# Hybrid encoder trunk, one core: a token-major projection behind every convolution projection

## The chip, the core and the metric

The kernel runs on one core of one Trainium2 chip, in one launch. The metric is the device time of one execution in microseconds, as the median of the runs; less is better. Work is spread over TensorE (PE in the profile, its weight loads PEld), VectorE (DVE), ScalarE (ACT), GpSimd (POOL) and the queue of SyncE (SP), which only issues DMAs here.

## What is computed

Two layers (DEPTH 2) over 256 tokens of width 1024. Each layer normalises its input, projects it with one wide matrix, runs two token mixers on pieces of the projection, and joins them:

```python
for l in range(DEPTH):
    h = rmsnorm(x, norm_w[l])
    proj = h @ w_in[l]
    (q_a, k_a, v_a, ab_a, z_a, q_b, k_b, v_b, z_b,
     gate_a, gate_b) = jnp.split(proj, SPLIT_IDX, axis=-1)
    y_a = gated_delta_branch(q_a, k_a, v_a, ab_a, z_a, conv_w[l], a_log[l], dt_bias[l], gdn_norm_w[l])
    lambda_init = 0.8 - 0.6 * math.exp(-0.3 * l)
    y_b = diff_attention_branch(q_b, k_b, v_b, z_b, cos, sin, diff_lambda[l], diff_subln_w[l], lambda_init)
    merged = (jax.nn.sigmoid(gate_a) * (y_a @ w_pa[l])
              + jax.nn.sigmoid(gate_b) * (y_b @ w_pb[l]))
    x = x + merged @ w_out[l]
return rmsnorm(x, final_norm_w)
```

The first branch (a) sends q, k and v through a convolution of 5 taps along the tokens and a SiLU, and runs a gated delta rule in both directions. In chunked form that rule needs, for every head and chunk, the inverse of a unit triangular matrix:

```python
L = jnp.where(strict, jnp.einsum('bhncd,bhnmd->bhncm', kb, k) * decay, 0.0)
T = lax.linalg.triangular_solve(eye + L, jnp.broadcast_to(eye, L.shape),
                                left_side=True, lower=True, unit_diagonal=True)
```

The second branch (b) rotates part of q and k (rotary positions), takes the difference of two softmax attentions per head, and multiplies by v.

## The kernel before, in words

**Projections.** All of them use the normalised input held transposed in `hT` as a high and a low float32r part, and weights that are split on the chip: per tile of 256 rows by 512 columns, SP issues a load of 512 KB into `raw`, ACT casts it to `hi` (L223), and DVE forms the rest `lo` (L225). `raw` has three buffers, `hi` and `lo` two each, so a weight tile can be made only two tiles ahead of PE. Three products (hi by hi, hi by lo, lo by hi) make one result. There are two forms. `proj_fm` (L279, feature-major, called by `conv`) has the weights stationary: 96 matmuls of 128x256 (L289, L291, L293) into the tiles `pf_k`, `pf_q` or `pf_v`, for 512 channels. `proj_tm` (L230, token-major) has the tokens stationary: 48 matmuls of 128x512 (L237 to L239) into tiles named `pp_...`, for 512 columns.

**After a convolution projection** DVE has much to do: for each of four blocks of 128 channels ACT scales the middle tap (L508), DVE adds the four other taps straight out of PSUM (L512, four instructions, tiles `cvk`, `cvq`, `cvv`), ACT takes a tanh (L516, `thk`, `thv`), DVE forms the SiLU (L521), and PE turns the result token-major (L529, `ctk`, `ctq`, `ctv`). A PSUM bank is given back only when the taps of both its blocks are added. **After a token-major projection** there is less: v's half (`vb_part`) is two copies on ACT (L343, out of `pp_vb`); q and k of branch b (`qk_part`, arguments: 0 for q or 1 for k, and the half of the heads) are a copy on ACT (L439, `stg`), four small rotations on DVE (L444 to L447) and transposes (L450, `qkt`), twice.

**PSUM.** The accumulators of projections and the attention scores share four banks (tag `p`, `banks2`); each projection and each head takes two.

**The chain of the triangular inverse.** With k's norms known, `log_decays` and `decays` make the decays; `weigh_k` forms A out of them and of k's products (L596, L620); `turn_blocks` sends A's diagonal blocks through DRAM; after q's second half `take_blocks` (L649) turns one copy of them on DVE, and `substitute` runs 31 dependent steps of two DVE instructions each (L655, L656, tiles `fstmp` and `X`). `spread_blocks` then copies the result on DVE (L659, `lt`), GpSimd writes it to DRAM (L663) and reads it back into the places that PE needs (L685 tile `T`, L689 tile `U_`), and `merges` builds the full inverse from the 32x32 blocks on PE (L703 `y64p`, L715 `zt`, L720 `z`, then L737 and L745), for two groups of four heads. `chunks` uses it.

**Heads of branch b.** `head(h)` makes scores on PE (L816, tiles `sc`, two banks, one for each of the two softmaxes), maxima on DVE (L823, `mx`), exponentials on ACT (L825, `es`), their difference on DVE (L828 to L833), transposes (L836, `at`) and the product with v (L842, `av`). Between them stand the projections `z_part` (tiles `pp_zb` and `pp_za`), whose result DVE takes through L304; then come the gates `pp_gb`, `pp_ga` and the products `pp_pb`, `pp_pa`.

**What sets the order.** The body of a layer is a list of calls written by hand (L859 to L900). A scheduler then orders the instructions of each engine when the program is built, by the order of the calls and by modelled times, so that pieces of later calls come ahead where it finds room; it also picks the banks and buffers. On the chip every engine's list runs in that fixed order. The first token-major half of v stands ahead of the list (`proj_by_tile`, L357).

Of the kernel before, what the change touches and what calls it, by code (L numbers as in the profile page):

```python
# [50 lines left out]
def hybrid_encoder(  # L51
# [178 lines left out]
    def proj_tm(act, w, c0, n, evac, nm, places=(None,) * 4):  # L230

        accs = banks2(f"pp_{nm}")
        for kt, hi, lo in weights(w, c0, n, nm, places):
            for m in range(NM):
                ts_ = slice(m * P, (m + 1) * P)
                o = accs[m][:, :n]
                T.matmul(o, act[kt // 4][:, 0, kt % 4, ts_], hi, start=kt == 0, stop=False)  # L237
                T.matmul(o, act[kt // 4][:, 0, kt % 4, ts_], lo, start=False, stop=False)  # L238
                mark["proj"] = T.matmul(o, act[kt // 4][:, 1, kt % 4, ts_], hi, start=False,  # L239
                                        stop=kt == KT - 1).ins  # L240
        for m in range(NM):
            evac(m, accs[m][:, :n])
# [91 lines left out]
    for l in range(DEPTH):  # L334
# [6 lines left out]
        def evac_v(i):  # L341
            def evac(m, ps):
                S.copy(vb[i][:, m, :], ps)  # L343
            return evac
# [111 lines left out]
        def vb_part(i):  # L456
            proj_tm(hT, wl, C_VB + 512 * i, 512, evac_v(i), f"vb{l}{i}")
# [164 lines left out]
        def weigh_q(g, c):  # L622
            bv = B[:, c, 4 * g : 4 * g + 4]
            V.tensor_tensor(bv, gram("kq", g, c, 1).unsqueeze(2).to_broadcast([P, 4, 2, P]), bv, ALU.mult)
# [21 lines left out]
        def take_blocks():  # L646

            with tc.issue_after(mark["conv"]):
                V.tensor_copy(la[64:P], lt[64:P].rearrange("p j i -> p i j"))  # L649
# [207 lines left out]


        conv("k", C_KA, 0, 0)  # L859
        conv("k", C_KA, 0, 1)  # L860
        vb_part(1)
        log_decays()
        conv("q", C_QA, 1, 0)
        qk_part(0, 0)
        decays(0, 0)
        weigh_k(0, 0)
        decays(0, 1)
# [7 lines left out]
        weigh_q(0, 1)  # L875
        conv("q", C_QA, 1, 1)
        take_blocks()
        qk_part(0, 1)
        weigh_q(1, 0)
        weigh_q(1, 1)  # L880
        substitute(0, 31)
        spread_blocks()
        conv("v", C_VA, None, 0)
        qk_part(1, 0)
        conv("v", C_VA, None, 1)
        qk_part(1, 1)
        head(0)
        z_part(zb, C_ZB, "zb", 0)
        head(1)
# [143 lines left out]
```

## Time and profile before

| quantity | value |
|---|---|
| median of 3 runs | 797.72 us (795.93 to 799.87) |
| span of the profiled execution | 798.2 us |
| what lies around it | the span is 0.5 us above the median of the runs |
| instructions | 13819 |
| moved by DMA | 126.92 MB |
| first layer's convolution stage, k's first group to the first head | about 28 to 177 us |
| second layer's | about 422 to 570 us |

Times within the trace are counted from the start of the span. A busy share is an average over stages; an engine's idle time is put down, in the view of waits, to what released it. An instruction's duration includes its latency: matmuls that follow each other overlap, and DVE's instructions begin some 0.08 us before the one ahead of them is shown to end.

### The profile page before, as it was taken

The numbers are of one execution on the slowest core, as the hardware profiler recorded it, in microseconds if no ns is written. First come the engines' busy times: TensorE is split into PE (matmuls) and PEld (weight loads), VectorE is DVE, ScalarE is ACT, GpSimd is POOL, SyncE is SP. The second block draws the span as 40 slices with busy tenths as digits, with TensorE's granted clock in tenths as the row PEclk, the third lists the DMA queues.
The fourth block names the chain that finished last, engine by engine and source line by source line (L and its number), as shares of the span: only waits on it lengthen the run. The fifth ranks groups of instructions, "written<-read, shape, count | busy, mean of one in ns | idle before, by whom it ended". The sixth has DMA issues, their size and how long they took to land.

```text
span 798.2 us, 13819 instructions
## 1 busy us (share of the span) xinstructions
PE 766.4 (96%) x5224; PEld 654.0 (82%) x5224; DVE 559.3 (70%) x1054; ACT 478.5 (60%) x1043; POOL 109.5 (14%) x149
## 2 busy tenths in 40 slices
PE   8989999999998999999989899999999999999996
PEld 4989889887876888878769798799778789887875
DVE  5487878999972653476655977889999436546564
ACT  5458776556775745654534786765667586446443
POOL 6000471100050100100010014501001401001000
PEclk9999999999998999999999999999999999999999
DMA  7455756554484544355754566566455734344551
GB/s 205 152 167 158 224 158 200 172 161 130 133 212 87 158 139 126 107 171 184 234 156 135 153 179 222 159 173 181 134 159 150 194 109 158 115 128 125 188 190 74
DMA packets 65842, 126.92 MB, mean 159 GB/s; under 512 B 7391, under 2 KB 7727, under 8 KB 65776
## 3 DMA queue, kind: packets, MB, share of 16 engines
q1 hardware_dynamic: 61198, 114.69, 47.4%
q0 software_dynamic: 4576, 11.35, 5.9%
q8 instruction: 41, 0.67, 0.4%
q14 instruction: 25, 0.20, 0.1%
q10 hardware_dynamic: 2, 0.00, 0.0%
HBM read 121.27 MB, written 4.75 MB: 158 GB/s over the span
## 4 chain that ended last, share of the span: by engine, by line
PE 66%; DVE 13%; DMA 9%; ACT 6%; issue 3%; POOL 3%; SPq 0%; POOLq 0%; ACTq 0%; DVEq 0%
PE pp_vb L274 3%; PE pp_qk L238 2%; PE pp_qk L239 2%; PE pp_qk L237 2%; DMA U__96<-udr 2%; PE pf_v L289 2%; PE pp_gb L237 2%; PE pf_v L293 2%; PE pf_v L291 2%; PE pp_gb L238 2%; PE pp_gb L239 2%; PE pp_pb L238 2%; PE pp_pb L237 2%; PE pp_pb L239 2%; PE pf_k L293 2%
## 5 line engine op out<-in xcount | busy, mean ns | idle before, releaser
L238 PE MATMUL pp_qk<-lo_qk,hT 128*128 128x512 f32 x128 | 51.3, 401 | 1.0 <-DVE lo_qk L225 1.0
L239 PE MATMUL pp_qk<-hi_qk,hT 128*128 128x512 f32 x128 | 50.1, 391 | 0.0
L237 PE MATMUL pp_qk<-hi_qk,hT 128*128 128x512 f32 x128 | 46.1, 398 | 1.1 <-ACT hi_qk L223 1.1
L225 DVE TENSOR_TENSOR lo_qk<-raw_qk,hi_qk 128x1024 fp32r<-128x1024 f32 x32 | 40.2, 1256 | 9.0 <-ACT hi_qk L223 8.7
L223 ACT CAST hi_qk<-raw_qk 128x1024 fp32r<-128x1024 f32 x32 | 33.5, 1046 | 20.0 <-PE pp_qk L239 10.8
L225 DVE TENSOR_TENSOR lo_pb<-raw_pb,hi_pb 128x1024 fp32r<-128x1024 f32 x16 | 19.6, 1224 | 33.6 <-ACT hi_pb L223 33.6
L289 PE MATMUL pf_q<-hT,hi_q 128*128 128x256 f32 x128 | 36.3, 288 | 1.3 <-ACT hi_q L223 1.2
L225 DVE TENSOR_TENSOR lo_gb<-raw_gb,hi_gb 128x1024 fp32r<-128x1024 f32 x16 | 19.6, 1223 | 25.2 <-ACT hi_gb L223 25.2
L289 PE MATMUL pf_v<-hT,hi_v 128*128 128x256 f32 x128 | 36.5, 288 | 0.0
L291 PE MATMUL pf_v<-hT,hi_v 128*128 128x256 f32 x128 | 36.2, 285 | 0.0
L825 ACT ACTIVATE es<-sc,mx 128x256 f32<-128x256 f32 x64 | 29.9, 475 | 10.4 <-DVE mx L823 10.3
L291 PE MATMUL pf_q<-hT,hi_q 128*128 128x256 f32 x128 | 35.8, 284 | 0.0
L289 PE MATMUL pf_k<-hT,hi_k 128*128 128x256 f32 x128 | 35.6, 283 | 0.0
L291 PE MATMUL pf_k<-hT,hi_k 128*128 128x256 f32 x128 | 35.6, 283 | 0.0
L293 PE MATMUL pf_q<-hT,lo_q 128*128 128x256 f32 x128 | 35.2, 290 | 0.1
L293 PE MATMUL pf_v<-hT,lo_v 128*128 128x256 f32 x128 | 34.6, 285 | 0.0
L293 PE MATMUL pf_k<-hT,lo_k 128*128 128x256 f32 x128 | 34.3, 286 | 0.0
L225 DVE TENSOR_TENSOR lo_pa<-raw_pa,hi_pa 128x1024 fp32r<-128x1024 f32 x16 | 19.6, 1224 | 17.9 <-ACT hi_pa L223 17.9
L225 DVE TENSOR_TENSOR lo_k<-raw_k,hi_k 128x1024 fp32r<-128x1024 f32 x16 | 19.6, 1222 | 17.6 <-ACT hi_k L223 17.6
L512 DVE SCALAR_TENSOR_TENSOR cvk<-pf_k,cw,cvk 128x254 f32<-128x254 f32 (+1 forms) x64 | 29.2, 478 | 2.0 <-ACT cvk L508 1.2
L223 ACT CAST hi_pa<-raw_pa 128x1024 fp32r<-128x1024 f32 x16 | 16.9, 1055 | 22.4 <-PE pp_pa L239 18.9
L223 ACT CAST hi_pb<-raw_pb 128x1024 fp32r<-128x1024 f32 x16 | 16.8, 1050 | 22.4 <-PE pp_pb L239 17.9
(367 smaller groups left out, 2550.6 us busy)
## 6 DMA issues: line engine op xcount, KB each, us to landing
raw_qk<-in_w_in_dram SPq DMA_DIRECT2D x32, 512.0 KB, 3.7
raw_vb<-in_w_in_dram SPq DMA_DIRECT2D x16, 512.0 KB, 4.1
raw_k<-in_w_in_dram SPq DMA_DIRECT2D x16, 512.0 KB, 3.8
raw_q<-in_w_in_dram SPq DMA_DIRECT2D x16, 512.0 KB, 3.7
raw_v<-in_w_in_dram SPq DMA_DIRECT2D x16, 512.0 KB, 4.0
raw_zb<-in_w_in_dram SPq DMA_DIRECT2D x16, 512.0 KB, 3.6
raw_za<-in_w_in_dram SPq DMA_DIRECT2D x16, 512.0 KB, 3.9
raw_gb<-in_w_in_dram SPq DMA_DIRECT2D x16, 512.0 KB, 4.4
```

What stands on the lines that cost most here:

```text
L223: S.copy(hi[:, :, :n], raw[:, :, :n])
L225: V.tensor_tensor(lo[:, :, :n], raw[:, :, :n], hi[:, :, :n].bitcast(F32), ALU.subtract)
L237: T.matmul(o, act[kt // 4][:, 0, kt % 4, ts_], hi, start=kt == 0, stop=False)
L238: T.matmul(o, act[kt // 4][:, 0, kt % 4, ts_], lo, start=False, stop=False)
L239: mark["proj"] = T.matmul(o, act[kt // 4][:, 1, kt % 4, ts_], hi, start=False, stop=kt == KT - 1).ins
L274: mark["proj"] = T.matmul(o, a_, w_, start=kt == 0 and a_ is ah and w_ is hi, stop=kt == KT - 1 and a_ is al).ins
L289: T.matmul(o, hi[:, cs], act[kt // 4][:, 0, kt % 4, :], start=first, stop=False, skip_group_check=True)
L291: T.matmul(o, hi[:, cs], act[kt // 4][:, 1, kt % 4, :], start=False, stop=False, skip_group_check=True)
L293: T.matmul(o, lo[:, cs], act[kt // 4][:, 0, kt % 4, :], start=False, stop=done, skip_group_check=True)
L512: V.scalar_tensor_tensor(ca[:, o0:o1], acc[:, b, o0 + sft : o1 + sft], cw[:, j, cb : cb + 1], ca[:, o0:o1], ALU.mult, ALU.add)
L825: S.activation(es[:, n, qt, :], spv[:, qt, :], AF.Exp, bias=mx[:, n, qt : qt + 1], accum_out=s_all[:, h, n, qt : qt + 1])
```

## The change

It moves four calls in the hand-written list, in both layers, and adds or removes no operation. v's second half goes from behind k's second group to between k's two groups. The rotated halves of q and k each go one place ahead: the first to behind k's second group, the others to between and behind q's and v's groups. Behind v's second group no token-major projection is left, and the first attention head follows it.

```diff
         conv("k", C_KA, 0, 0)
+        vb_part(1)
         conv("k", C_KA, 0, 1)
-        vb_part(1)
+        qk_part(0, 0)
         log_decays()
         conv("q", C_QA, 1, 0)
-        qk_part(0, 0)
+        qk_part(0, 1)
         decays(0, 0)
...
         conv("q", C_QA, 1, 1)
         take_blocks()
-        qk_part(0, 1)
+        qk_part(1, 0)
         weigh_q(1, 0)
         weigh_q(1, 1)
         substitute(0, 31)
         spread_blocks()
         conv("v", C_VA, None, 0)
-        qk_part(1, 0)
+        qk_part(1, 1)
         conv("v", C_VA, None, 1)
-        qk_part(1, 1)
         head(0)
```

The scheduler makes of it the following, in three places of the first layer; the second layer is alike. In names, `vb` is branch b's v, `k` is branch a's k, and numbers tell one buffer from another.

DVE, while the first group of k is taken out of PSUM (blocks `cvk_513` and `cvk_522` are its last two; `cvk_663` belongs to k's second group), before:

```order
L225 TENSOR_TENSOR lo_vb_740<-raw_vb_741,hi_vb_739 128x1024
L521 SCALAR_TENSOR_TENSOR kq_336<-thk_519,cvk_513 128x2x128
L512 SCALAR_TENSOR_TENSOR cvk_522<-pf_k_364,cw_274,cvk_522 128x254
L512 SCALAR_TENSOR_TENSOR cvk_522<-pf_k_364,cw_274,cvk_522 128x255
L512 SCALAR_TENSOR_TENSOR cvk_663<-pf_k_541,cw_274,cvk_663 128x254
L512 SCALAR_TENSOR_TENSOR cvk_522<-pf_k_364,cw_274,cvk_522 128x255
L512 SCALAR_TENSOR_TENSOR cvk_663<-pf_k_541,cw_274,cvk_663 128x255
```

And after (`lo_k_680` and `lo_k_710` are weights of k's second group, whose taps now come later):

```order
L225 TENSOR_TENSOR lo_k_650<-raw_k_651,hi_k_649 128x1024
L521 SCALAR_TENSOR_TENSOR kq_336<-thk_519,cvk_513 128x2x128
L512 SCALAR_TENSOR_TENSOR cvk_522<-pf_k_364,cw_274,cvk_522 128x254
L512 SCALAR_TENSOR_TENSOR cvk_522<-pf_k_364,cw_274,cvk_522 128x255
L225 TENSOR_TENSOR lo_k_680<-raw_k_681,hi_k_679 128x1024
L512 SCALAR_TENSOR_TENSOR cvk_522<-pf_k_364,cw_274,cvk_522 128x255
L512 SCALAR_TENSOR_TENSOR cvk_522<-pf_k_364,cw_274,cvk_522 128x254
L225 TENSOR_TENSOR lo_k_710<-raw_k_711,hi_k_709 128x1024
```

The taps of two groups no longer stand among each other; weights stand between them.

PE, where the last projection of the convolution stage ends and the first head and `z_part` begin, before (`sc_2116` holds the scores whose bank the second half of `pp_zb`'s accumulators takes over; the first takes a bank that `pp_qk` left):

```order
L238 MATMUL pp_qk_2014<-lo_qk_2070,hT_1_113 128x512
L239 MATMUL pp_qk_2014<-hi_qk_2069,hT_1_113 128x512
L816 MATMUL sc_2116<-qkT_0_298 128x256
L816 MATMUL sc_2115<-qkT_0_298 128x256
L816 MATMUL sc_2116<-qkT_0_298 128x256
L816 MATMUL sc_2115<-qkT_0_298 128x256
L237 MATMUL pp_zb_2147<-hi_zb_2149,hT_0_112 128x512
```

And after (one score stands further ahead, inside v's second group):

```order
L291 MATMUL pf_v_1944<-hT_1_113,hi_v_2035 128x256
L293 MATMUL pf_v_1944<-hT_1_113,lo_v_2036 128x256
L816 MATMUL sc_2115<-qkT_0_298 128x256
L816 MATMUL sc_2116<-qkT_0_298 128x256
L816 MATMUL sc_2115<-qkT_0_298 128x256
L529 MATMUL ctv_1837<-ident,thv_1834 128x128 x2
L237 MATMUL pp_zb_2147<-hi_zb_2149,hT_0_112 128x512
```

The head now follows v's second group, and both accumulators of `pp_zb` lie in banks that the head's scores hold; the built program puts `sc_2116` and `pp_zb_2147` into one bank.

PE, where the merges begin, before (`2501` and `2571` belong to the first group of heads, `2536` to the second):

```order
L703 MATMUL y64p_2536<-T_2490,A_346 32x32 x32
L715 MATMUL zt_2571<-U__96,y_2502 32x32 x2
L842 MATMUL av_2819<-vb_1_140,aT_2811 128x128 x4
L239 MATMUL pp_za_3016<-hi_za_3071,hT_1_113 128x512
L836 MATMUL at_3110<-ident,es_3093 128x128 x4
L715 MATMUL zt_2571<-U__96,y_2502 32x32 x30
L720 MATMUL z_2572<-y_2502,U__96 32x32 x16
L816 MATMUL sc_3130<-qkT_1_299 128x256
```

And after:

```order
L842 MATMUL av_2819<-vb_1_140,aT_2811 128x128
L238 MATMUL pp_za_3016<-lo_za_3072,hT_1_113 128x512
L239 MATMUL pp_za_3016<-hi_za_3071,hT_1_113 128x512
L836 MATMUL at_3110<-ident,es_3093 128x128 x4
L816 MATMUL sc_3130<-qkT_1_299 128x256
L816 MATMUL sc_3129<-qkT_1_299 128x256
L703 MATMUL y64p_2536<-T_2490,A_346 32x32 x32
L715 MATMUL zt_2571<-U__96,y_2502 32x32 x2
L842 MATMUL av_3119<-vb_1_140,aT_3111 128x128 x4
L720 MATMUL z_2572<-y_2502,U__96 32x32 x16
L237 MATMUL pp_gb_3218<-hi_gb_3220,hT_0_112 128x512
```

The product `av_2819`, the last of `pp_za`, the transposes `at_3110` and the last head's four scores (the piece leaves out their second pair) now stand ahead of the first `zt`, and 24 matmuls of `pp_gb` behind it.

## The prediction

> **What bounds the kernel now.** I read the page first, then PE's waits, then the stages by windows, then the places where PE waits, by the timeline. The page:
>
> ```profile
> span 798.2 us, 13819 instructions
> PE 766.4 (96%) x5224; PEld 654.0 (82%) x5224; DVE 559.3 (70%) x1054; ACT 478.5 (60%) x1043; POOL 109.5 (14%) x149
> PE 66%; DVE 13%; DMA 9%; ACT 6%; issue 3%; POOL 3%; SPq 0%; POOLq 0%; ACTq 0%; DVEq 0%
> raw_qk<-in_w_in_dram SPq DMA_DIRECT2D x32, 512.0 KB, 3.7
> ```
>
> PE is busy for 96% and the chain runs through it for 66%. The change leaves PE's work as it is, so it can only win or lose idle time and clock. Weights land in 3.7 us, and no wait below is on one: the four loads of a moved projection move with it in SP's queue and cost nothing. Where PE waits, over both layers:
>
> ```profile
> PE zt L715 <- DMA U__96<-udr: 3.3, 2, 1.9
> PE pp_vb L237 <- DVE cvk L512: 3.1, 2, 1.5
> PE y64p L703 <- DMA T<-udr: 2.8, 2, 2.5
> PE pp_vb L238 <- DVE lo_vb L225: 0.9, 2, 0.5
> PE pp_zb L237 <- ACT es L825: 0.9, 2, 0.5
> ```
>
> Two of the rows belong to v's second half behind both of k's groups: it wants the bank of k's first group, whose taps DVE has not yet read. The `zt` and `y64p` rows belong to the merges, which wait for the DMAs behind the substitution. Stages of 12 us (columns: time, busy PE, PEld, DVE, ACT, POOL, granted clock, DMA share, GB/s):
>
> ```profile
> 52.00:64.00 12.00, 9.85 (x47) 7.43 (x47) 10.84 (x22) 9.37 (x28) 0.00 (x0) 1.00 0.37 104
> 64.00:76.00 12.00, 12.00 (x90) 11.41 (x89) 9.06 (x15) 8.38 (x19) 0.00 (x0) 1.00 0.66 203
> 184.00:196.00 12.00, 12.00 (x63) 9.37 (x62) 11.48 (x21) 8.38 (x20) 0.00 (x0) 1.00 0.49 139
> ```
>
> The reader is to see two kinds of stage. At 52 to 64 PE loses 2.15 us. At 184 to 196, under the heads, PE loses nothing, but DVE is full, because the substitution fills it. DVE decides there when the copy `lt` comes, and with it T and U.
>
> **The change, part by part.**
>
> *1. v's half between k's groups.* Under each token-major projection DVE has room for the taps of the group ahead, and its bank has been free for a whole projection. Both `pp_vb` rows should go: 4.0 us. Each of their four waits also costs the overlap with the matmul ahead, about 0.16 us, which is a duration of 0.39 less a distance of 0.227 (six matmuls start in 23.85 - 22.49 = 1.36 us):
>
> ```profile
> 22.49 1.52 PE L274 MATMUL pp_vb<-wktm_vb,hT 128*128 128x512 f32 x6
> 23.85 0.62 PE L274 MATMUL pp_vb<-wvtm_vb,hT 128*128 128x512 f32 x2
> ```
>
> That makes 4.0 + 4 x 0.16 = 4.6 us, 2.3 per layer; with small waits that the view leaves out I take 2.5. Late next is ACT: the copies of v's half stand there ahead of the cast of k's second weight tile. The cover is k's first tile, 24 matmuls of 128x256; if it is too small, the wait only moves, and the gain is nothing. The same change of form from q's second qk half to v's first group shows no wait now, so I take the gain in full.
>
> *2. The head behind v's second group.* Rows at the end of the convolution stage, and the copy:
>
> ```profile
> 163.17 0.47 ACT L508 ACTIVATE cvv<-pf_v,cw 128x256 f32<-128x256 f32 x1 [1.17 <-PE pf_v L293]
> 163.67 0.48 DVE L512 SCALAR_TENSOR_TENSOR cvv<-pf_v,cw,cvv 128x254 f32<-128x254 f32 x1 [0.26 <-ACT cvv L508]
> 175.27 1.75 PE L816 MATMUL sc<-qkT 64*128 64x256 f32 x8
> 179.33 1.27 DVE L823 TENSOR_REDUCE mx<-sc 128x2 f32<-128x512 f32 x2
> 180.04 0.47 ACT L825 ACTIVATE es<-sc,mx 128x256 f32<-128x256 f32 x1 [0.45 <-DVE mx L823]
> 181.11 0.50 PE L237 MATMUL pp_zb<-hi_zb,hT 128*128 128x512 f32 x1 [0.48 <-ACT es L825]
> 556.11 0.47 ACT L508 ACTIVATE cvv<-pf_v,cw 128x256 f32<-128x256 f32 x1 [1.17 <-PE pf_v L293]
> 572.27 1.28 DVE L823 TENSOR_REDUCE mx<-sc 128x2 f32<-128x512 f32 x2
> L659 DVE COPY lt<-X x2: 1103/1114/1124, 219.8 to 612.5; 128x1024 f32<-128x1024 f32 x2
> 179.30:219.80 40.50, 40.02 (x210) 31.53 (x210) 39.24 (x91) 28.51 (x74) 0.00 (x0) 1.00 0.45 130
> ```
>
> ACT's L508 at 163.17 marks the end of v's first accumulator. DVE took its first tap 0.5 us later, so it is not behind there. In the new order `mx` follows two taps and one substitution row, or the scores themselves: 1.7 us behind that mark. From `mx` to the first `pp_zb` it takes 181.11 - 179.33 = 1.8 us as now, in all 3.5. PE's cover is the last six products of v, three scores at 0.44 (1.75 over four) and two transposes: about 2.2. So PE waits 1.3 us where it waited 0.45 per layer: +0.9 (bounds 0 to 3).
>
> *3. DVE's queue up to the copy.* Before, v's last taps ran under `pp_qk`; now they run under the heads, where DVE is full. Between the first `mx` and the copy 90 DVE rows stood and 112 stand now, by counting the two orders: 10 more taps, 8 more substitution rows, 2 more `lo`, 2 `es`, 2 `thv`, one `vtm`, one `cc`, less 4 rotation rows. Their durations:
>
> ```profile
> L225 DVE TENSOR_TENSOR lo_zb<-raw_zb,hi_zb 128x1024 fp32r<-128x1024 f32 x6 | 7.3, 1218 | 0.5 <-ACT hi_zb L223 0.5
> L656 DVE TENSOR_TENSOR X<-X,fstmp 128x247 f32<-128x247 f32 (+15 forms) x19 | 6.7, 351 | 0.1
> L833 DVE SCALAR_TENSOR_TENSOR es<-es,cc 128x256 f32<-128x256 f32 x8 | 3.5, 477 | 0.0
> L512 DVE SCALAR_TENSOR_TENSOR cvv<-pf_v,cw,cvv 128x254 f32<-128x254 f32 (+1 forms) x4 | 1.9, 469 | 0.0
> L532 DVE TENSOR_TENSOR vtm<-ctv,nrm 128x512 f32<-128x512 f32 x2 | 1.4, 677 | 0.0
> L521 DVE SCALAR_TENSOR_TENSOR thv<-thv,cvv 128x256 f32<-128x256 f32 x2 | 0.8, 412 | 0.0
> ```
>
> 10 x 0.47 + 8 x 0.35 + 2 x 1.22 + 2 x 0.48 + 2 x 0.41 + 0.68 = 12.4; the `cc` row and the four rotation rows are small (some -0.8 together), and each of 22 rows overlaps its neighbour by 0.08: about 10 us net. The way from `mx` to the copy took 40.5 us with DVE busy for 39.24. It becomes 49.2 if DVE idles no more and 50.5 if it idles as now; I take 49.6, nearer the first, as more work is queued.
>
> The weights `lo` of `pp_zb` and `pp_za` stand in that queue too. The third `lo` of `pp_zb`'s second half has 25.7 us of DVE rows between it and `mx` (19.5 before, both added up as above), and PE, at 0.227 a product, wants it 23.5 us behind `mx`: PE waits 1 to 2 us for DVE there. This lies ahead of the merges, so it counts only if PE were the later one at that meeting.
>
> `log_decays` and `decays`, with their rows on POOL and their DMAs, come one projection later, together with q's groups. From q's first group to the copy of `take_blocks` the four lists of rows read as before, one projection on; I cost that at nothing.
>
> *4. The merges, where the two meet.* PE's rows there:
>
> ```profile
> 242.17 0.83 PE L703 MATMUL y64p<-T,A 32*32 32x32 f32 x64 [2.55 <-DMA T<-udr]
> 244.39 0.32 PE L715 MATMUL zt<-U__96,y 32*32 32x32 f32 x4 [1.39 <-DMA U__96<-udr]
> 244.63 2.08 PE L842 MATMUL av<-vb,aT 128*128 128x128 f32 x8
> 246.93 1.05 PE L836 MATMUL at<-ident,es 128*128 128x128 f32 x4
> 634.87 0.25 PE L715 MATMUL zt<-U__96,y 32*32 32x32 f32 x4 [1.91 <-DMA U__96<-udr]
> ```
>
> U releases `zt` 244.4 - 219.8 = 24.6 us behind the copy in the first layer and 22.4 in the second, and PE is waiting by then in both. So this wait ends last, and what PE gains in step 1 is spent here unless the copy moves as well. The copy follows v's end. Ahead of v's end stand one more half of 48 matmuls at 0.227 (10.9 us), and about 1.3 us of transposes and one score; the wait of step 1 is gone: +9.7. First layer: 163.17 + 9.7 + 1.7 + 49.6 = 224.2, against 219.8: 4.4 later. Second: 556.11 + 9.7 + 1.7 + 49.6 = 617.1, against 612.5: 4.6 later. Against this PE has more work done when `zt` is released: four scores (1.75), one `av` and one `at` (half of 2.08 + 1.05, since they ran at clock 0.50) and a `pp_za` matmul (0.23), 3.5 us. That leaves +0.9 and +1.1. PE itself would be there by about 241, so its own delays of steps 2 and 3 are covered.
>
> The clock behind those two waits, in windows of 2 us (the granted clock is the column ahead of the DMA share):
>
> ```profile
> 243.00:245.00 2.00, 0.61 (x5) 0.58 (x6) 0.00 (x0) 0.37 (x1) 0.00 (x0) 0.50 0.93 219
> 245.00:247.00 2.00, 2.00 (x10) 1.82 (x10) 0.00 (x0) 0.26 (x1) 0.00 (x0) 0.50 0.19 60
> 636.00:638.00 2.00, 2.00 (x10) 1.68 (x9) 0.00 (x0) 0.88 (x2) 0.00 (x0) 0.50 0.50 140
> ```
>
> It is at half, and stays there for some 5 us behind the release in the first layer and 4 in the second. The wait grows to about 6 us, but the clock has gone down already, so I leave this cost as it is (bounds -2 to +2 in all). [...]
>
> *5. Behind the merges* the second group's `z` now stands next to the following step (L737), with 24 matmuls fewer between. No row prices that: 0 to 2 us per layer; I take 0.25, since the other chunk steps show no wait.
>
> **The sum:** 798.2 + 0.9 + 1.1 + 0.5 = 800.7 of span. The span lies 0.5 above the median of the runs (797.72), so 800.2: **800 us**, no change that can be told. A measurement of this kernel tells about 0.5% from none, 4 us: 793.7 and 801.7.
>
> **Rivals.**
>
> *A. DVE makes it up, faster.* The way from `mx` to the copy, or from the copy to U, is shorter by 3.6 us than I have it (46 instead of 49.6; the two layers differ by 2.2 us in the DMA part alone). Then the copy stands 0.8 to 1 us later than before against 3.5 us of work moved, and some 2.6 per layer of PE's gains are kept: 797.7 - 5.2 = 792.5. For it: DVE is at 9.06 of 12 at 64 to 76, so it could start the heads with nothing queued. Against: it is full from there on. 0.15.
>
> *B. The copy is later still, slower.* Under the heads DVE and PE hang on each other: a late `lo` holds PE for 2 us, and then DVE waits for the scores and the `pp_zb` that PE brings late. The way is 50.5 + 2 = 52.5 instead of 49.6: 2.9 per layer, 800 + 5.8 = 806. It decides from a copy that stands 5.4 us later than before, as every us beyond 4.5 counts in both layers. For it: DVE at 11.48 of 12. Against: DVE was not behind at 163.67. 0.27.
>
> *C. The wait of step 1 moves to k's second group*, onto ACT's casts. Then the copy is 2.5 later in each layer: 800 + 5 = 805. Against it: no wait at the like places. 0.08.
>
> The forecast itself, a copy 3.5 to 5.4 us later of which the moved rows make up the most, gets 0.50; its own range is 798 to 802.
>
> **Chances.** Faster by over 0.5% is A: 0.15. Slower by over 0.5% is B, C and a little of the forecast's upper end: 0.27 + 0.08 + 0.03 = 0.38. Within: 0.47. The range for 8 in 10 takes in B and C with a us for what they leave out, and of A the nearer part: 794 to 807.
>
> **What would show it.** Right: no `pp_vb` wait on `cvk`; a wait of `pp_zb` on `es` above 1 us; DVE over 11.5 of 12 from the first head on; the copy at about 224 and 617; `zt` waiting for U some 5 us. Wrong: the copy within 2 us of where it was, or PE at `zt` without a wait (A); the copy beyond 226 (B); waits at `pf_k` in k's second group (C).

## The result, and the profile after

The changed kernel takes 810.52 us (median of 4 runs, 808.59 to 813.09) against 798.8 for the kernel before (4 runs, 795.93 to 800.9): a ratio of 1.0157, 95% interval 1.0127 to 1.0188. It is slower, and lies above the 794 to 807 us that were forecast. The profiled execution is the fastest of the four; in each of them the time is 1.8 us above the span. If the same lies around the span before (798.2), that profile is the execution of 799.87 us, one of the slower ones: so the spans differ by 8.6 us and the medians by 11.7. From the page:

```profile
span 806.8 us, 13826 instructions
PE 772.0 (96%) x5224; PEld 657.1 (81%) x5224; DVE 561.1 (70%) x1054; ACT 478.1 (59%) x1043; POOL 108.3 (13%) x149
```

The share of PE is what it was, 96%, and tells nothing of the loss: a matmul at half clock counts as busy, and for longer (0.63 us for a `pp_zb` matmul at granted clock 0.50, 0.39 at 1.00). Where PE waits (both layers; us in total, times, longest):

```profile
PE pp_zb L237 <- DVE zb L304: 3.5, 2, 1.8
PE z L720 <- DMA U__96<-udr: 3.1, 2, 2.2
...
PE av L842 <- ACT aT L838: 2.9, 2, 1.5
PE pp_zb L237 <- ACT es L825: 2.5, 2, 1.3
PE zt L715 <- DMA U__96<-udr: 2.2, 2, 1.2
...
PE pp_pa L237 <- ACT yaT L194: 1.4, 1, 1.4
```

Both `pp_vb` rows are gone, as forecast, and the wait on `es` is 1.3 us per layer, as forecast. Two rows are new under the heads: `pp_zb`'s second half waits until DVE has taken the first half out of its bank (L304), and `av` waits until ACT has copied the head's transposes (L838). At the merges the waits for T and U come to 6.2 us, where they were 6.1, but half of them now stand at `z`, which waited for nothing before.

To add these up, the windows view cuts each layer at k's first matmul, v's last, 3 us ahead of the first `y64p`, and the end of L745: the convolutions, the heads, the merges (columns as in the prediction: time, busy PE, PEld, DVE, ACT, POOL, granted clock, DMA share, GB/s). The kernel before:

```profile
21.40:163.60 142.20, 138.38 (x950) 125.87 (x949) 111.85 (x223) 92.14 (x210) 28.95 (x32) 1.00 0.58 173
163.60:230.40 66.80, 66.32 (x341) 52.38 (x340) 63.01 (x139) 45.91 (x115) 4.22 (x8) 1.00 0.54 157
230.40:265.00 34.60, 30.42 (x554) 24.85 (x553) 13.89 (x24) 21.12 (x55) 8.16 (x14) 0.90 0.54 128
...
413.30:556.50 143.20, 138.64 (x949) 125.85 (x948) 111.79 (x211) 88.69 (x204) 27.29 (x32) 1.00 0.58 168
556.50:623.00 66.50, 66.05 (x340) 52.12 (x338) 62.93 (x139) 45.84 (x114) 5.43 (x10) 1.00 0.55 160
623.00:654.90 31.90, 29.99 (x555) 24.52 (x553) 13.60 (x21) 21.22 (x56) 6.38 (x11) 0.95 0.54 130
```

The changed kernel:

```profile
20.30:172.80 152.50, 150.49 (x1008) 136.26 (x1006) 120.57 (x242) 98.73 (x218) 27.62 (x32) 1.00 0.59 177
172.80:238.60 65.80, 61.31 (x311) 47.48 (x311) 59.99 (x131) 42.81 (x115) 7.43 (x15) 0.97 0.49 139
238.60:274.70 36.10, 32.96 (x553) 26.79 (x551) 11.27 (x19) 22.33 (x57) 8.04 (x9) 0.86 0.57 131
...
418.20:568.90 150.70, 149.64 (x1008) 135.97 (x1006) 118.55 (x225) 95.27 (x212) 27.38 (x32) 1.00 0.59 173
568.90:634.60 65.70, 61.22 (x311) 47.45 (x310) 60.09 (x131) 42.78 (x113) 7.34 (x14) 0.97 0.49 140
634.60:668.20 33.60, 30.43 (x553) 24.81 (x551) 11.97 (x22) 22.43 (x57) 7.58 (x9) 0.95 0.58 136
```

Two numbers come from each row: PE's idle time (the length less PE's busy time) and what half clock takes (1 less the granted clock, times the length). Under the first layer's heads that is 65.8 - 61.31 = 4.5 and 0.03 x 65.8 = 2.0, where it was 0.5 and nothing. Added over both layers, with the stretch from the merges to `w_out` as a fourth column (clock 1.00, PE idle for 1 to 2 us), PE loses:

| us, both layers | convolutions | heads | merges | rest | sum | span less sum |
|---|---|---|---|---|---|---|
| before | 8.4 | 1.0 | 11.2 | 2.1 | 22.7 | 775.5 |
| after | 3.1 | 13.0 | 13.1 | 3.3 | 32.5 | 774.3 |

The last column is nearly the same: the ledger holds what the change did, to within 1.2 us. It won 5.3 us in the convolutions and lost 12 under the heads, 1.9 in the merges and 1.2 behind them. The places under the first layer's first heads (timeline):

```profile
173.92 0.68 DVE L823 TENSOR_REDUCE mx<-sc 128x2 f32<-128x512 f32 x1
175.71 0.63 PE L237 MATMUL pp_zb<-hi_zb,hT 128*128 128x512 f32 x1 [1.27 <-ACT es L825]
193.38 0.68 DVE L304 SCALAR_TENSOR_TENSOR zb<-zb,pp_zb 128x512 f32<-128x512 f32 x1
194.11 0.50 PE L237 MATMUL pp_zb<-hi_zb,hT 128*128 128x512 f32 x1 [1.76 <-DVE zb L304]
```

At this first maximum 21 DVE rows of v (L512, L521, L532, 10.4 us in all) are still to come ahead of the copy; in the kernel before there were 8 (4.1 us). The copy behind the substitution, which the prediction put at 224.2 and 617.1, stands here:

```profile
L659 DVE COPY lt<-X x2: 1058/1062/1065, 225.5 to 621.6; 128x1024 f32<-128x1024 f32 x2
```

The first layer starts 1.1 us earlier than before (k's first matmul at 20.3 against 21.4) and the second 4.9 later (418.2 against 413.3). Counted from there the copy is 6.8 and 4.2 us later than before; 4.4 and 4.6 were forecast.

### The profile page after: what moved, and what is told of

The parts are those of the page before. It is cut to its first block, busy times and chain, and to the rows that moved or that the text cites. A ratio compares the mean times of both kernels' runs of the same rounds, so it can differ in the third digit from the quotient of the medians.

```text
span 806.8 us, 13826 instructions
## 1 busy us (share of the span) xinstructions
PE 772.0 (96%) x5224; PEld 657.1 (81%) x5224; DVE 561.1 (70%) x1054; ACT 478.1 (59%) x1043; POOL 108.3 (13%) x149
## 4 chain that ended last, share of the span: by engine, by line
PE 71%; DMA 9%; DVE 9%; ACT 5%; issue 2%; POOL 2%; SPq 0%; POOLq 0%; ACTq 0%; DVEq 0%
PE pp_qk L238 3%; PE pp_qk L239 3%; PE pp_qk L237 3%; PE pp_vb L274 3%; DMA raw_q<-in_w_in_dram 3%; DMA U__96<-udr 2%; PE pp_gb L237 2%; PE pp_gb L238 2%; PE pp_gb L239 2%; PE pf_k L293 2%; PE pf_v L289 2%; PE pf_k L291 2%; PE pf_k L289 2%; PE pf_v L293 2%; PE pf_v L291 2%
## 5 line engine op out<-in xcount | busy, mean ns | idle before, releaser
L225 DVE TENSOR_TENSOR lo_qk<-raw_qk,hi_qk 128x1024 fp32r<-128x1024 f32 x32 | 40.2, 1257 | 10.7 <-ACT hi_qk L223 10.6
L225 DVE TENSOR_TENSOR lo_gb<-raw_gb,hi_gb 128x1024 fp32r<-128x1024 f32 x16 | 19.6, 1224 | 33.9 <-ACT hi_gb L223 33.5
L825 ACT ACTIVATE es<-sc,mx 128x256 f32<-128x256 f32 x64 | 29.7, 474 | 18.1 <-DVE mx L823 18.1
L225 DVE TENSOR_TENSOR lo_pb<-raw_pb,hi_pb 128x1024 fp32r<-128x1024 f32 x16 | 19.6, 1224 | 29.4 <-ACT hi_pb L223 29.3
L225 DVE TENSOR_TENSOR lo_ga<-raw_ga,hi_ga 128x1024 fp32r<-128x1024 f32 x16 | 19.5, 1225 | 24.5 <-ACT hi_ga L223 24.5
L237 PE MATMUL pp_zb<-hi_zb,hT 128*128 128x512 f32 x64 | 25.8, 424 | 6.0 <-DVE zb L304 3.5
L512 DVE SCALAR_TENSOR_TENSOR cvk<-pf_k,cw,cvk 128x254 f32<-128x254 f32 (+1 forms) x64 | 29.8, 478 | 2.6 <-ACT cvk L508 1.9
L223 ACT CAST hi_pb<-raw_pb 128x1024 fp32r<-128x1024 f32 x16 | 16.8, 1053 | 24.6 <-PE pp_pb L239 15.3
L225 DVE TENSOR_TENSOR lo_k<-raw_k,hi_k 128x1024 fp32r<-128x1024 f32 x16 | 19.6, 1224 | 16.8 <-ACT hi_k L223 16.5
```

The costliest lines, as they stand in the source:

```text
L223: S.copy(hi[:, :, :n], raw[:, :, :n])
L225: V.tensor_tensor(lo[:, :, :n], raw[:, :, :n], hi[:, :, :n].bitcast(F32), ALU.subtract)
L512: V.scalar_tensor_tensor(ca[:, o0:o1], acc[:, b, o0 + sft : o1 + sft], cw[:, j, cb : cb + 1], ca[:, o0:o1], ALU.mult, ALU.add)
L825: S.activation(es[:, n, qt, :], spv[:, qt, :], AF.Exp, bias=mx[:, n, qt : qt + 1], accum_out=s_all[:, h, n, qt : qt + 1])
```

## The experiments

Each ratio is to the kernel before, run beside the kernel in question. The ledger is made as above from each kernel's own windows, of one execution, which lies up to 4.4 us from its kernel's median (number 5's is the furthest); span less sum lies between 771 and 779 us in all of them, and in the three with idle matmuls as well once these are taken off. "Copy" is the time from k's first matmul to the copy in each layer.

| kernel | ratio (95%) | convolutions, heads, merges, rest | copy |
|---|---|---|---|
| before | 1 | 8.4, 1.0, 11.2, 2.1 | 198.4, 199.2 |
| after | 1.0157 (1.0127 to 1.0188) | 3.1, 13.0, 13.1, 3.3 | 205.2, 203.4 |
| 1 v's half alone | 1.0205 (1.0182 to 1.0228) | 16.3, 0.8, 11.3, 2.0 | 203.8, 201.8 |
| 2 q and k halves alone | 1.0199 (1.0159 to 1.0238) | 14.0, 8.6, 9.9, 1.5 | 206.0, 205.7 |
| 3 q's half behind take_blocks | 0.9974 (0.9954 to 0.9994) | 7.6, 5.2, 4.3, 2.4 | 198.7, 200.3 |
| 4 z_b ahead of the head | 1.0117 (1.0087 to 1.0147) | 3.1, 12.9, 17.3, 1.2 | 200.7, 200.4 |
| 5 k's half behind four heads | 1.0227 (1.0194 to 1.0260) | 7.2, 20.1, 12.5, 2.3 | 193.2, 194.5 |
| 6 number 3, z_b ahead | 1.0013 (0.9995 to 1.0032) | 5.9, 6.6, 6.1, 2.4 | 194.0, 193.0 |
| 7 after, 23 steps | 1.0032 (1.0005 to 1.0059) | 2.9, 7.9, 14.6, 1.5 | 194.2, 192.6 |
| 8 before, 23 steps | 0.9934 (0.9910 to 0.9959) | 7.5, 1.0, 6.1, 2.2 | 186.4, 186.5 |
| 9 one wait filled | 1.0090 (1.0059 to 1.0121) | 3.9, 10.4, 9.5, 3.3 | 205.6, 204.4 |
| 10 four waits filled | 1.0114 (1.0086 to 1.0142) | 2.9, 3.8, 9.2, 2.2 | 202.3, 202.1 |
| 11 number 3, merges filled | 0.9979 (0.9959 to 1.0000) | 7.2, 3.2, 5.2, 2.1 | 198.1, 198.5 |
| 12 lo on GpSimd | 1.0194 (1.0167 to 1.0222) | 4.3, 12.2, 17.4, 1.0 | 203.1, 203.4 |
| 13 after, two taps fewer | 0.9905 (0.9880 to 0.9931) | 4.1, 5.8, 2.6, 2.4 | 202.1, 201.3 |
| 14 before, two taps fewer | 1.0092 (1.0062 to 1.0123) | 7.4, 0.0, 18.1, 2.2 | 198.2, 198.2 |
| 15 after, L624 later | 1.0019 (1.0006 to 1.0033) | 5.1, 10.2, 6.1, 2.5 | 206.2, 207.3 |
| 16 number 3, L624 later | 1.0029 (1.0011 to 1.0047) | 9.1, 1.0, 13.0, 2.1 | 199.0, 200.0 |

**The parts of the change (1, 2, 3).** Number 1 is the kernel before with the `vb_part` line of the change alone:

```diff
         conv("k", C_KA, 0, 0)
+        vb_part(1)
         conv("k", C_KA, 0, 1)
-        vb_part(1)
         log_decays()
```

> Only v's second half moves between k's two groups; the rotated halves stay as in the kernel before, so k's second group and q's first group now follow each other and the head comes behind a rotated half again. If the four banks are what made the old wait, the pair that follows each other has only moved: the first rotated half then waits for the bank of k's second group, 2 to 2.5 us per layer, and the time is that of before within 2 us. If the wait was special to v's half (its copies, its weights), nothing waits there, both layers gain 2.5 to 4 us, and the time is 5 to 8 us below before. Neither theory lets the copy behind the substitution be late: its way from the first maximum is about 40 us as before.

Neither: nothing waits for a bank of k's second group, but the convolutions lose 7.9 us more than before, and the span is 8.6 us longer. k's second group now runs straight into `log_decays` and q, and PE waits for A and for the weights on DVE, and for `stg` on ACT:

```profile
PE kk L596 <- DVE A L620: 5.9, 3, 2.0
...
PE pp_qk L238 <- DVE lo_qk L225: 3.2, 7, 0.7
PE pf_q L289 <- ACT stg L439: 2.3, 2, 1.1
```

Number 2 is the changed kernel with `vb_part(1)` put back behind k's second group.

> The changed kernel, but with v's second half behind k's second group as before: two pairs of groups follow each other, k's two and v's second with the head. If the two parts of the change simply add, the time is that of the changed kernel plus the 6 to 8 us that it gained in its first part: 16 to 20 us above before. If the late start of the heads gives DVE room (the rival), a part of that is taken up by the waits under the heads and at the merges, and the time is only 12 to 14 us above before.

Some 15 us above the kernel before, between the two expectations. That is 0.42% above the changed kernel, about 3 us, with intervals that overlap: what v's half between k's groups is worth when a rotated half follows k can't be told from nothing. Number 3 puts back the q and k halves but the first:

```diff
         conv("q", C_QA, 1, 0)
-        qk_part(0, 1)
         decays(0, 0)
...
         take_blocks()
-        qk_part(1, 0)
+        qk_part(0, 1)
...
         conv("v", C_VA, None, 0)
-        qk_part(1, 1)
+        qk_part(1, 0)
         conv("v", C_VA, None, 1)
+        qk_part(1, 1)
         head(0)
```

> The changed kernel with the second rotated half of q behind take_blocks again, and the halves of k behind v's groups, as in the kernel before: in front of the substitution only v's half and one rotated half are left, k's groups are still apart, and q's two groups follow each other. Theory stage (from take_blocks to the copy DVE is full, 80 of 82 us, so the copy comes that much behind take_blocks, and the change has made take_blocks late by a projection of 10.9 us for which DVE there is spared only about 2.7): take_blocks comes 2 to 4 us earlier than in the kernel before, the copy too, nothing waits under the heads, and the time is 4 to 7 us below before. Theory pair (two groups that follow each other cost the same wherever they stand): 2 to 3 us per layer are lost again between q's groups, as in the first run of v's half alone, and the time is that of before or up to 10 us above.

2 us faster than before: less than the 4 to 7 of the first theory, and without the loss of the second. q's pair does wait a little (`pp_qk` on `lo_qk` 3.0 us in five places; 1.0 in two before). With numbers 1 to 3 the loss is put: three projections ahead of `take_blocks` instead of two, with the head straight behind v, cost 1.8 to 2.0%, with k's groups split (0.9974 to 1.0157) or together (1 to 1.0199).

**Is it the place, or the amount of work in the stage (4, 5, 6)?** Number 4 swaps `head(0)` and the first `z_part` in the changed kernel.

> The changed kernel with the first half of z_b ahead of the first head, so that a token-major projection stands behind v's second group again. The waits of pp_zb on es (1.3 us per layer) go. Theory copy (the late copy sets the merges, and what PE loses under the heads would be lost at the merges anyway): the time falls only by what the copy comes earlier, about 2 us per layer, to 6 to 8 us above before. Theory heads (the waits under the heads, 5 us per layer with their half clock, add up by themselves): they all go, and the time is 0 to 3 us above before.

The waits on `es` are gone, but PE waits for scores instead (`sc` on `zb` 3.2 us, on `cvv` 1.3), and the heads cost as much. Number 5 is number 3 with `qk_part(1, 1)` moved from ahead of `head(0)` to behind `head(3)`.

> As the kernel with q's second rotated half behind take_blocks (0.997 of before), but with k's second rotated half behind the fourth head instead of behind v's second group. The first head follows v's second group directly, as in the changed kernel; the number of token-major projections between take_blocks and the merges is that of the kernel before. Theory cover (what counts is how much of PE's work lies beside DVE's full stage): the first pp_zb waits for es again, 1 to 1.5 us per layer, but the merges wait less, and the time is 0.995 to 1.003 of before. Theory place (the head directly behind v's second group is what costs): PE loses the 5 us per layer under the heads as in the changed kernel, and the time is 1.008 to 1.014.

The theory of cover falls. As much of PE's work lies in the stage as before, and its median is the highest of all, above the range of the other theory too. The windows of the heads and the merges, and the copy:

```profile
162.30:238.40 76.10, 71.15 (x335) 54.93 (x334) 63.91 (x140) 44.31 (x109) 11.79 (x20) 0.93 0.60 152
238.40:264.50 26.10, 24.40 (x517) 19.12 (x515) 11.99 (x22) 18.77 (x52) 0.58 (x1) 0.87 0.36 105
561.80:637.40 75.60, 71.08 (x334) 54.95 (x334) 63.86 (x139) 44.23 (x109) 11.81 (x20) 0.93 0.58 153
```

```profile
L659 DVE COPY lt<-X x2: 1134/1135/1136, 214.2 to 613.6; 128x1024 f32<-128x1024 f32 x2
```

The copy comes 5 us earlier in its layer than in the kernel before, and yet PE loses 10 us under the heads of each layer (5.0 idle and 5.3 of half clock in the first). So a late copy is not needed for a loss: in this kernel no DMA ends a wait of PE at `zt`, PE itself comes last there. Number 6 is number 3 with the swap of number 4.

> As the kernel with q's second rotated half behind take_blocks, and with the first half of z_b ahead of the first head. Theory cover: the same work lies in the stage, so the time stays within 0.3 per cent of that kernel's 0.997. Theory place: more token-major work between v and the head helps as it did when z_b was set ahead in the changed kernel (1.016 to 1.012), and the time falls to 0.992 to 0.994.

Slightly slower than number 3, and just outside what either theory had: where a rotated half already stands between v and the head, more token-major work there doesn't help. Why is not shown.

**The substitution (7, 8).** Both have `substitute(0, 23)`; the last 8 steps are left out, so the inverse is not complete.

> The changed kernel with the last 8 of the 31 steps of the substitution left out, so the inverse is not complete; 16 DVE rows of 0.29 us with 0.08 of overlap, 3.4 us, go ahead of the copy and nothing else. Theory copy: the copy, U and the merges come 3.4 us earlier in each layer, and the time falls by 5 to 7 us against the changed kernel, to 5 to 7 us above before. Theory heads: the waits of pp_zb on es and on zb lie ahead of these rows, so they stay, and the time falls by 0 to 2 us, to 10 to 12 above before.

> The kernel before with the last 8 of the 31 steps of the substitution left out, so the inverse is not complete. Theory stage: DVE has some 4 us less to do between take_blocks and the copy, the copy comes 4 to 5 us earlier in each layer, and the waits at the merges (4.4 us in the first layer, 1.9 in the second, with the half clock behind them) shrink: 4 to 8 us below before. If only the changed kernel hangs on the chain, the time is that of before within 2 us.

The changed kernel gains about 1.2%, the kernel before 0.7%. The changed kernel's gain is more than the 5 to 7 us that the theory of the copy had. That speaks for the copy, but the heads' loss falls too, from 13.0 to 7.9, which is not what that theory says; and the built order changed with it: GpSimd's reads of U now come ahead of those of T.

**The clock (9, 10, 11).** Idle matmuls on tiles that nobody reads, in the changed kernel behind the scores of the first head:

```diff
+            if h == 0:
+                wm = bank(f"wm{l}")
+                for _ in range(6):
+                    with behind(mm.ins):
+                        mm = T.matmul(wm, hT[0][:, 0, 0, 0:P], hT[0][:, 0, 0:2, :], start=True, stop=True)
```

> The changed kernel with six idle matmuls of 128x512 behind the first head's scores, whose result nobody reads, in the place where PE waits for es; they should keep the clock at 1.00 behind that wait. Theory stage: DVE sets the pace under the heads, so the 1.8 us that the half clock cost the first pp_zb of the first layer go into the next wait for DVE, and the time stays that of the changed kernel within 1.5 us. Theory heads: the half clock under the heads costs by itself, and the time falls by 2 to 4 us.

Faster by some 5 us (1.0157 to 1.0090), more than expected of either. Behind the wait on `es` the windows of the changed kernel read:

```profile
176.00:178.00 2.00, 2.00 (x6) 1.51 (x6) 2.00 (x7) 1.02 (x4) 0.00 (x0) 0.50 0.53 116
178.00:180.00 2.00, 2.00 (x8) 1.60 (x7) 2.00 (x7) 0.78 (x2) 0.00 (x0) 0.67 0.38 146
```

and with the wait filled:

```profile
176.00:178.00 2.00, 2.00 (x11) 1.60 (x10) 2.00 (x5) 1.00 (x5) 0.00 (x0) 1.00 0.27 29
178.00:180.00 2.00, 2.00 (x11) 1.64 (x10) 2.00 (x8) 1.13 (x4) 0.00 (x0) 1.00 0.64 234
```

Eleven matmuls in 2 us instead of six. In number 10 eight more stand behind the second head's scores, and eight of 128x256 each ahead of `zt` and of `z`.

> The changed kernel with idle matmuls in four places where PE waits, per layer: six of 128x512 behind the first head's scores, eight behind the second head's, eight of 128x256 ahead of zt and eight ahead of z in the merges; nobody reads their results. One such fill (the first) brought the time from 1.016 to 1.009 of before. If the half clock behind the other waits costs as much again, the mean granted clock rises from 0.983 to above 0.993 and the time falls to 1.001 to 1.005. If the other waits stand on DVE and DMA whatever the clock, the fills change the clock but not the time: 1.007 to 1.013.

The clock rises to 0.993, the heads' loss falls to 3.8, but the fills take 10.2 us themselves (28 of 0.227 and 32 of 0.12), and `y64p` now waits 3.0 us per layer for T: the time doesn't follow the clock any further. Number 11 has the fills of the merges in number 3.

> As the kernel with q's second rotated half behind take_blocks, with the eight idle matmuls of 128x256 ahead of zt and eight ahead of z in the merges. There that kernel waits about 1 us and falls to half clock in one layer of its profile. If half clock at the merges costs, the time falls from 0.997 to 0.993 to 0.996; if the fill only takes PE's time, it rises by 2 to 4 us, to 0.999 to 1.002.

No difference to number 3.

**DVE's rows at v's end (12 to 16).** Number 12 takes every second low part of z_b's weights off DVE (L225):

```diff
-                    V.tensor_tensor(lo[:, :, :n], raw[:, :, :n], hi[:, :, :n].bitcast(F32),
-                                    ALU.subtract)
+                    (G if nm[:2] == "zb" and kp % 2 else V).tensor_tensor(
+                        lo[:, :, :n], raw[:, :, :n], hi[:, :, :n].bitcast(F32), ALU.subtract)
```

> The changed kernel with the low part of every second weight tile of z_b formed on GpSimd instead of DVE: 4 rows of 1.22 us per layer go from DVE's full stage, nothing else is left out. Theory stage: the copy comes 4 to 5 us earlier than in the changed kernel, the waits of PE under the heads shrink by as much as GpSimd's rows allow, and the time falls to 3 to 6 us above before. If GpSimd's rows (1.64 us for half that size in another place, so some 3.3) hold PE, a wait of pp_zb on lo from GpSimd of 1 to 2 us per tile takes the place, and the time is that of the changed kernel, 10 to 13 above before.

Nothing gained, for a reason that neither theory had: a step of the substitution on DVE beside such a part on GpSimd takes 1.80 us instead of 0.41, and the substitution's rows take 26.7 us in the first layer instead of 20.7. The same row in the changed kernel, beside no work on GpSimd, and in number 12:

```profile
187.26 0.41 DVE L655 TENSOR_TENSOR fstmp<-la,X 128x247 f32<-128x247 f32 x1
```

```profile
186.95 1.80 DVE L655 TENSOR_TENSOR fstmp<-la,X 128x247 f32<-128x247 f32 x1
```

GpSimd's row beside it, 185.97 to 188.47:

```profile
185.97 2.50 POOL L225 TENSOR_TENSOR lo_zb<-raw_zb,hi_zb 128x1024 fp32r<-128x1024 f32 x1 [7.81 <-ACT hi_zb L223]
```

Numbers 13 and 14 leave out two of the four shifted taps of v's second group (L512), so the convolution of half of v is not complete:

```diff
-                    for j in (0, 1, 3, 4):
+                    for j in (0, 4) if seg == "v" and g == 1 else (0, 1, 3, 4):
```

> The changed kernel with two of the four shifted taps left out in v's second group (so the convolution of half of v is not complete): 8 DVE rows of 0.47 us per layer go that stand between v's end and the first maxima or among the first heads' rows; 13 instead of 21 rows of v are left at the first maximum, where the kernel before has 8. Theory backlog (DVE comes to the first head with v's taps still to do, and PE pays for them in waits on es, on zb and on aT and in half clock): the distance to the kernel before with the same taps left out shrinks from 1.6 per cent to 0.8 or less, and the waits under the heads to about half. Theory copy (the end of the substitution sets the merges): both kernels gain alike from 3.3 us less of DVE work, and the distance stays at 1.3 to 1.8 per cent.

> The kernel before with the same two taps of v's second group left out, as the other half of the comparison. Theory backlog: there the taps run under the rotated half of k, where PE does not wait, so little is gained: 0 to 3 us by the earlier copy. Theory copy: the copy comes 3 us earlier in each layer, and 3 to 6 us are gained, as much as in the changed kernel.

The two part: the changed kernel gains 2.5% and is faster than the kernel before with all its taps, while the kernel before loses 0.9%. Its own heads lose nothing now, but its merges lose 18.1 instead of 11.2, with the copy where it was (198.2), as DVE stands idle for 4.6 us between `take_blocks` and the copy instead of 2.2. The changed kernel with fewer taps, heads and merges:

```profile
173.60:236.10 62.50, 59.64 (x312) 46.66 (x312) 57.27 (x123) 42.93 (x115) 7.53 (x15) 1.00 0.52 147
236.10:265.10 29.00, 27.02 (x548) 22.34 (x546) 12.91 (x28) 20.07 (x53) 7.98 (x9) 1.00 0.65 158
560.60:623.20 62.60, 59.74 (x312) 46.68 (x312) 57.28 (x123) 42.96 (x115) 7.65 (x15) 1.00 0.53 148
623.20:651.40 28.20, 27.62 (x548) 22.48 (x547) 12.96 (x28) 20.01 (x53) 7.24 (x8) 1.00 0.64 160
```

The wait on `zb` is gone, those on `es` and `aT` stay (1.4 and 1.5 us per layer), and the clock no longer falls in either stage. Numbers 15 and 16 leave nothing out. They call two DVE rows, L624 of the second group of heads, later:

```diff
-        weigh_q(1, 0)
-        weigh_q(1, 1)
         substitute(0, 31)
...
         z_part(za, C_ZA, "za", 0)
+        weigh_q(1, 0)
+        weigh_q(1, 1)
         in_step(merges(0), merges(1))
```

> The changed kernel with two DVE rows per layer (L624 of the second group of heads, 1.2 us each) called behind the first half of z_a instead of behind take_blocks; the built order puts them behind the second head. Nothing is left out, and both stay ahead of the copy. Theory backlog: DVE is 2.4 us further at the first head (three quarters of what the two omitted taps were worth), the waits of pp_zb on es and zb shrink, and the time falls from 1.016 to 1.003 to 1.010 of before. Theory copy: as many rows stand ahead of the copy as before, it comes when it did, and the time stays at 1.013 to 1.019.

> As the kernel with q's second rotated half behind take_blocks (0.997 of before), with the same two rows of L624 called behind the first half of z_a. Theory backlog: PE hardly waits for DVE at the first heads there (0.8 us per layer), so at most that is gained: 0.994 to 0.998. If the two rows only meet the heads' own rows in their new place, PE waits there instead and the time is 0.999 to 1.005.

Number 15 comes back to 1.0019, but not in the way expected: the waits on `es` and `zb` are as long as before (2.9 and 3.1 us), and the copy is later still (206.2 and 207.3). What fell are the merges, from 13.1 to 6.1. In the second layer the built order now holds 17 matmuls of `pp_gb` ahead of `zt` and `z`, where the changed kernel has none and waits; from its timeline:

```profile
636.83 1.16 PE L842 MATMUL av<-vb,aT 128*128 128x128 f32 x8
638.04 0.50 PE L237 MATMUL pp_gb<-hi_gb,hT 128*128 128x512 f32 x1
...
642.68 0.39 PE L237 MATMUL pp_gb<-hi_gb,hT 128*128 128x512 f32 x1
643.24 0.22 PE L715 MATMUL zt<-U__96,y 32*32 32x32 f32 x2
```

So a late copy is not enough for the loss either. In number 16 the rows cost a little where there was nothing to gain.

## Why the prediction was wrong, step by step

*1, v's half between k's groups: right, as a part of the whole change.* 2.5 us per layer forecast; the convolutions lose 1.8 and 3.5 us less, 5.3 in all. By itself the move wins nothing: in number 1 the convolutions lose 7.9 us more than before, in waits that the step did not look at.

*2, the head behind v's second group: the wait right, its price not.* PE waits 1.27 us for `es` in both layers; 1.3 was forecast. In the first layer the clock falls to half behind it, for 3.4 us (175.9 to 179.3), which had no term.

*3, DVE's queue: right up to the copy, wrong in who waits.* The way from `mx` to the copy is 51.6 us; 49.6 was taken, 50.5 was the end of the range, rival B had 52.5. The copy stood at 225.5, 1.3 late. PE's waits for DVE under the heads were put at 1 to 2 us, on a late `lo`, and said to count "only if PE were the later one at that meeting". None on `lo` shows; PE waits 1.76 us on `zb` and, for ACT, 1.46 on `aT`. With those on `es` and the half clock the heads cost 6.0 us more per layer than before.

*4, the merges: right up to the release of `zt`, wrong behind it. This is the step that failed.* "PE itself would be there by about 241, so its own delays of steps 2 and 3 are covered": PE was there at 246.5, and U still came last, in both layers, though the wait for it was 1.2 and 1.0 us instead of some 5:

```profile
247.66 0.32 PE L715 MATMUL zt<-U__96,y 32*32 32x32 f32 x4 [1.21 <-DMA U__96<-udr]
251.19 1.06 PE L720 MATMUL z<-y,U__96 32*32 32x32 f32 x30 [0.97 <-DMA U__96<-udr]
642.47 0.25 PE L715 MATMUL zt<-U__96,y 32*32 32x32 f32 x4 [0.99 <-DMA U__96<-udr]
646.15 0.69 PE L720 MATMUL z<-y,U__96 32*32 32x32 f32 x30 [2.17 <-DMA U__96<-udr]
```

Counted from k's first matmul `zt` is released 4.4 and 2.7 us later than before; 4.4 and 4.6 were forecast. In the first layer that is luck in part: the copy is 6.8 later, and the way from it to U is 22.2 us instead of 24.6. (The "more work done" was too large as well: the four scores take 1.13 us at 243.63, and not the 1.75 of a row in which PE's matmuls stood further apart.) From the release of `zt` to the end of L745 the windows read, before and after:

```profile
244.39:264.96 20.57, 20.57 (x385) 17.50 (x385) 7.82 (x14) 15.04 (x41) 0.58 (x1) 0.88 0.32 98
634.87:654.90 20.03, 20.03 (x385) 16.95 (x385) 7.55 (x12) 15.05 (x41) 0.00 (x0) 0.91 0.38 106
247.66:274.70 27.04, 26.07 (x392) 21.36 (x392) 6.61 (x12) 16.81 (x41) 3.68 (x3) 0.81 0.40 107
642.47:668.20 25.73, 23.56 (x392) 19.27 (x392) 7.89 (x16) 17.59 (x43) 3.13 (x2) 0.93 0.42 112
```

By the ledger's two numbers PE loses 2.5 and 1.8 us there before, 6.1 and 4.0 after: 5.8 more, and 7.0 with the 1.2 of the rest. That is most of the 9.8 us by which the ledger grew. Ahead of the release it grew by 2.8, where the forecast had 0.9 and 1.1; behind it the forecast had nothing in this step and 0.5 in step 5.

Two things make the 5.8: 3.1 us are waits of `z`, 2.7 are half clock. First, `z` has lost its cover. Before, the last of `pp_za`, the transposes and most of `zt` stood between the first `zt` and `z`, and `z` came 4.2 and 4.0 us behind it without a wait; now one product stands there, `z` comes 2.3 and 1.3 us behind, and waits 0.97 and 2.17 us for a further read of U. The prediction counted work that moved ahead of `zt` as a gain and priced no wait at `z`. Second, it said of the half clock: "the clock has gone down already, so I leave this cost as it is". In the first layer it lasts 10.2 us (247.6 to 257.8) where it was 6.8, and from 252.2 on it lies on `pp_gb`, dense matmuls, for 5.6 us. Over both layers half clock takes 10.7 us by the windows, against 5.1.

The runs bear this out. In number 15 PE waits as long on `es` and `zb` as in the changed kernel, and the copy is later still, but the stretch behind `zt` loses only 0.6 us in the first layer and nothing in the second, and the time is nearly that of the kernel before. In number 13 the stretch loses nothing in either layer, and the kernel is 20 us faster than the changed one, with a copy only 2 to 3 us earlier. That delays under the heads are covered holds only as long as U comes last: with the early copy of number 5 they count in full.

*5, behind the merges:* 0.25 taken, 0 to 2 bounded. No wait stands at L737. The rest of the layer loses 1.1 and 0.1 us more, in the first layer with a wait of `pp_pa` on `yaT` (1.4).

*The sum:* the span was to be 800.7 and is 806.8. The median lies 3.7 above that: 1.8 lie around each span, and the profiled run is 1.9 below the median. Rival B was right in sign and in that DVE and PE hang on each other under the heads; its 806 falls 4.5 short of the median. It put the loss into the copy. Of its two tests, a copy 5.4 us later is met in the first layer (225.5 against 219.8) and a copy beyond 226 is not, and the copy is not where most of the loss stands. Rival C did not come: no wait stands at `pf_k`, nor does one in number 1.

*What stays open.* What each wait under the heads is worth by itself: filling one gave 5 us, filling four no more. Every edit also made the scheduler build another order at the merges, and the merges' loss moves by some 7 us with it (number 15 against the changed kernel, and number 14). No run changes the order between `zt` and `z` alone, so the split of the 5.8 us between the lost cover and the clock rests on the traces.

## What to carry to other kernels

Keep a ledger by stage of an engine's idle time plus what half clock takes; here it accounted for the span of eighteen profiles to within some 4 us, while the busy share stood at 95 to 97% throughout. Make it once more with a cut at the wait that the forecast takes for the last one. Here delays ahead of that cut were covered, and most of the loss lay behind it: work that is pulled ahead of a wait is taken away from behind it, where it may have covered the next wait (here `z` waited for U for 3.1 us, and for nothing before), and a half clock that was there before can last longer (here 10.2 us instead of 6.8). When work is moved out of a stage in which another engine is full, look at what that engine has queued at the stage's next boundary (here 21 rows of v's on DVE at the first maximum, 8 before), and not only at when its last result comes.

## What the runs showed of the hardware

In the changed kernel PE waits 1.27 us for `es` in both layers. In the first layer half clock follows (175.9 to 179.3), in the second it does not:

```profile
571.86 0.50 PE L237 MATMUL pp_zb<-hi_zb,hT 128*128 128x512 f32 x1 [1.27 <-ACT es L825]
175.90:179.30 3.40, 3.40 (x9) 2.62 (x9) 3.40 (x11) 1.80 (x6) 0.00 (x0) 0.50 0.53 154
571.86:575.30 3.44, 3.44 (x15) 2.87 (x16) 3.44 (x12) 1.73 (x6) 0.00 (x0) 1.00 0.52 152
```

With the wait on `zb` it is the other way round: 1.76 us at 194.11 leave the clock at 1.00, 1.75 at 588.68 are followed by half clock until 592.3. So the length of one wait doesn't tell; what does is not shown. The wait of 1.27 us at 175.71 stood alone: in the 54 us ahead of it PE had no other gap of more than 0.15 us. In the eighteen traces, read in windows of 2 us from 10 us on, each stretch of half clock, but for the one in which the trace ends, lasts 3.4 us or two or three times as much (6.8, 10.2). At a granted clock of 0.50 that makes 1.7 us of work, or a multiple, taken from a PE that has work to do; this is an estimate, half the length of the stretch.

In number 12 a DVE row with two operands in SBUF took 1.80 us (186.95) beside a subtraction of 128x1024 on GpSimd, and another, of 128x256, 1.60 (196.00) beside the next (194.69 to 197.32), where the changed kernel has 0.41 for each. A DVE row that reads PSUM, at 195.61 beside that second subtraction, kept its 0.47. What makes the difference is not shown.
